# Low parts of the dense weights: an accumulating DMA in place of a subtraction on VectorE

## The chip, the cores and the metric

The kernel runs on one core of a Trainium2 chip. The metric is the time of one execution on the device, in microseconds. The core has five engines with a queue of instructions each, and every queue is worked through in order: TensorE (PE in the profile, with its weight loads as PEld), VectorE (DVE), ScalarE (ACT), GpSimd (POOL) and SyncE (SP), which here only issues DMAs. Sixteen DMA engines move the data of all queues.

## The reference

One layer of a hybrid encoder, for 512 tokens of width 1024, all in float32. A normalised input is projected once to 11,272 columns, which feed two token mixers and two gates; each mixer's result is projected back, gated and summed, and a last projection is added to the input:

```python
h = rmsnorm(x, norm_w)
proj = jnp.einsum('bsd,de->bse', h, w_in) + b_in
(mq, mk, mv, mi, mf, mo, mz, sq, sk, sv, sz, gates) = jnp.split(proj, split_at, axis=-1)
...
qk = jax.nn.silu(causal_depthwise_conv(jnp.concatenate([mq, mk], axis=-1), conv_w, conv_b))
hm = mlstm_chunkwise(...)                      # 4 heads of 256
y_m = hm * jax.nn.sigmoid(mo) * jax.nn.silu(mz)
...
os_ = stick_breaking_attention(qs, ks_, ...)   # 8 heads of 128
y_s = os_ * jax.nn.silu(sz)
...
merged = (g_m * jnp.einsum('bse,ed->bsd', y_m, w_proj_m)
          + g_s * jnp.einsum('bse,ed->bsd', y_s, w_proj_s))
x = x + jnp.einsum('bsd,de->bse', merged, w_out)
```

## The kernel before

TensorE works on the type fp32r, which keeps fewer bits than float32. To keep the accuracy, every operand is split into a high part (the value, rounded by writing it as fp32r) and a low part (the value less the high part), and each product is three matmuls: high by high, high by low, low by high (`mm3`, lines 84 to 87, accumulating in PSUM). A product of two low parts is left out.

The dense projections are 112 units of work (`Unit`, line 94). A unit is one block of weights of 128 x 1024 elements, 512 KB. In a `chan_group` the block is eight tiles of 128 input rows by 128 output channels, which TensorE holds as weights while the 512 tokens stream through. In a `tok_group` it is two tiles of 128 rows by 512 columns, which stream while the tokens are held; four units make one group of 512 columns. Either way a unit is 24 matmuls of 128x512.

A unit passes through three steps. `load` (line 107) issues the DMA from SP into the staging tile `st` (tag `stg`, three buffers). `split` (line 111) takes tiles `wh` and `wl` (three buffers each) and calls the helper `split` of line 89: ACT copies `st` to `wh` (L90), then DVE writes `wl` as `st` less `wh` (L91). The helper is also used for other operands: transposed queries and keys, attention weights, the mixers' outputs and the merged tile. `mm` runs the 24 matmuls, in two halves.

The order of all instructions is written out by hand (`manual_schedule`); the loop at line 980 goes over the units. For unit c it issues, in this order: the evacuation of unit c-1 from PSUM (`evac`, on ACT and DVE); what was deferred to c; `ahead(c)`, which splits up to unit c+2 and loads up to unit c+4; the first half of c's matmuls; one step of each attention or mLSTM head that is under way (generators, `head`); the second half. In the mLSTM query and key groups an attribute `slow` puts `ahead(c)` before the evacuation. The first four units are split by a routine of their own (`first_split`), so 108 units go through `Unit.split`.

Around the dense units lie the steps that the prediction names. The query and key groups of the mLSTM end in a causal convolution (`qk_group` of `MPair`): ACT adds the bias (L621), DVE runs four taps (L624 and three times L626), ACT takes a sigmoid (L629), and two later units finish it (L632, L638, L642). An attention head's scores go through two sigmoids on ACT (L407, L411), two masks on POOL (L409, L412), a running product and a multiplication on DVE (L415, L416), and are transposed on TensorE (L440). An mLSTM head's weights are exponentials on ACT (L699), and its outputs are normalised by ACT copies (L748) before TensorE transposes them (L762). POOL also computes the row norms (L260, L261). No DMA is issued from POOL.

Of the kernel before, what the change touches and what calls it, by code (L numbers as in the profile page):

```python
# [11 lines left out]
AF = mybir.ActivationFunctionType  # L12
OP = mybir.AluOpType
# [21 lines left out]
def tile_hybrid_layer(  # L35
# [16 lines left out]
    nc = tc.nc  # L52
# [20 lines left out]
    def blk(tag, dt=F32, shape=(512,), name=None, p=128):  # L73

        where = mp if tag in MISC else sp
        return where.tile([p] + list(shape), dt, name=name or tag, tag=tag, bufs=BUFS[tag])
# [12 lines left out]
    def split(src, hi, lo):  # L89
        nc.scalar.activation(hi, src, AF.Copy)  # L90
        nc.vector.tensor_tensor(lo, src, hi.bitcast(F32), op=OP.subtract)  # L91


    class Unit:
# [16 lines left out]
        def split(self):  # L111
            self.wh = blk("wh", FR, self.shape)
            self.wl = blk("wl", FR, self.shape)
            split(self.st, self.wh, self.wl)

    units = []

# [187 lines left out]
    class SbSet:  # L305
# [70 lines left out]
        def head(self, h):  # L376
            hs = slice(h * 128, (h + 1) * 128)
            tr = []
            for name in ("q", "k"):
                tp = att_ps()  # L380
                for tb in range(TB):
                    nc.tensor.transpose(tp[:, tb * 128:(tb + 1) * 128], self.raw[name][tb][:, hs], ident)  # L382
                th = blk("qk", FR, name=name + "th")
                tl = blk("qk", FR, name=name + "tl")
                if name == "q":
                    nc.scalar.activation(th, tp, AF.Copy, scale=qkw)
                    nc.vector.scalar_tensor_tensor(tl, tp, qkw, th.bitcast(F32), op0=OP.mult, op1=OP.subtract)
                else:
                    split(tp, th, tl)
                tr.append((th, tl))  # L390
# [43 lines left out]
            def turn(js):  # L434
                tp = att_ps()
                at = 0
                for j in js:
                    n = T - j * 128
                    for i in range(j, TB):
                        nc.tensor.transpose(tp[:, at + (i - j) * 128:at + (i - j + 1) * 128],  # L440
                                            a_t[i][:, j * 128:(j + 1) * 128], ident)
                    at += n
                ap = blk("P5", FR, (2, 512), name="at_split")
                ah, al = ap[:, 0, :], ap[:, 1, :]
                split(tp[:, 0:at], ah[:, 0:at], al[:, 0:at])
                at = 0
                for j in js:
                    n = T - j * 128
                    a_parts[j] = ah[:, at:at + n], al[:, at:at + n]
                    at += n  # L450
# [140 lines left out]
    class MPair:  # L591
# [84 lines left out]
        def head(self, h):  # L676
# [27 lines left out]
            def score(js):  # L704
                sc = att_ps()
                at = 0
                for j in js:
                    lo = j * 128
                    for d in range(2):
                        mm3(sc[:, at:at + T - lo], kt[d][0][:, lo:lo + 128], kt[d][1][:, lo:lo + 128],  # L710
                            qt[d][0][:, lo:], qt[d][1][:, lo:], d == 0, d == 1)
                    at += T - lo
                o = P_OFF[js[0]]
                w = w_all[:, o:o + at]
                nc.vector.tensor_tensor(w, sc[:, 0:at], w, op=OP.mult)
                ph, pl = [t[:, o:o + at] for t in p_all]
                split(w, ph, pl)
                for j in js:
                    pp[j] = [t[:, P_OFF[j]:P_OFF[j] + T - 128 * j] for t in p_all]
# [325 lines left out]
```

## Time and profile before

| | |
|---|---|
| time, median of 2 runs | 719.12 us (718.85 to 719.39) |
| the profiled execution's own time | 720.13 us |
| its span | 718.4 us |
| granted TensorE clock, mean | 0.997 |
| TensorE busy | 709.8 us |
| VectorE busy | 424.5 us |
| ScalarE busy | 315.8 us |
| GpSimd busy | 93.5 us |
| DMA | 67.80 MB, mean 94 GB/s |

In the profile, L12 is line 12 of the kernel; where a helper records an operation, the line is the helper's, so the split of every operand is on L90 and L91 and is told apart by its tiles. A line of a group gives the line, the engine, the operation, the tiles written and read, the shape and the count, then the busy time in us and the mean of one in ns, then the engine's idle time just before and who ended it. A line of the timeline gives start and duration in us, and in brackets the idle time before. A line of the windows gives the stretch and its length, then busy time and count for PE, PEld, DVE, ACT and POOL, the granted clock, the share of the 16 DMA engines in use, and GB/s. A line of the waits gives who waited for whom, the total in us, the number of times and the longest. A line of the DMA issues ends with the median time from issue to landing.

### The profile page before, as it was taken

To read this page: it belongs to the slowest core of one execution; us is meant where nothing else is said; L and a number is where in the kernel's file an instruction comes from. 1 tells how busy PE (TensorE), PEld (TensorE's weight loads), DVE (VectorE), ACT (ScalarE), POOL (GpSimd) and SP (SyncE) were. 2 spreads that over 40 slices of the span, in tenths; PEclk is the share of its full clock that TensorE was granted. 3 is DMA by queue.
4 is the path that set the end of the run, shared out by engine and by line. 5 is a ranking of instruction groups with operands and counts; after the bars stand their busy time and mean duration, and the time that the engine had idled before them with its cause. 6 is when DMAs were issued, how large, how long until landed. Compare 5 with 4: busy or idle time off the path is not lost.

```text
span 718.4 us, 9058 instructions
## 1 busy us (share of the span) xinstructions
PE 709.8 (99%) x3356; PEld 593.1 (83%) x3356; DVE 424.5 (59%) x663; ACT 315.8 (44%) x601; POOL 93.5 (13%) x235
## 2 busy tenths in 40 slices
PE   7999999999999999999999999999999999999997
PEld 5888888888888888888888888888888888888886
DVE  5837886656487568279944737994343254556441
ACT  5245364476255544244475534447554343222210
POOL 5422022253022112000001110000112000000000
PEclk9999999999999999999999999999999999999999
DMA  6433332233323222333332233333223333333621
GB/s 239 133 103 81 109 86 77 69 95 92 99 62 87 58 86 62 102 91 97 101 94 59 63 99 88 91 100 89 74 59 89 89 91 97 104 88 89 234 89 58
DMA packets 91475, 67.80 MB, mean 94 GB/s; under 512 B 3470, under 2 KB 77608, under 8 KB 91432
## 3 DMA queue, kind: packets, MB, share of 16 engines
q1 hardware_dynamic: 91432, 67.23, 32.8%
q8 instruction: 26, 0.43, 0.2%
q14 instruction: 17, 0.14, 0.1%
HBM read 65.12 MB, written 2.10 MB: 94 GB/s over the span
## 4 chain that ended last, share of the span: by engine, by line
PE 97%; DMA 1%; DVE 1%; POOL 0%; SPq 0%; issue 0%; ACT 0%; DVEq 0%
PE dps L85 28%; PE dps L87 27%; PE dps L86 27%; PE aps L86 2%; PE aps L87 2%; PE aps L85 2%; PE aps L440 1%; PE aps L382 1%; DMA stg<-in_w_in_dram 1%; PE dps L934 1%; PE dps L932 1%; PE dps L933 1%; PE aps L735 1%; PE aps L736 1%; PE aps L737 1%; DVE fl L891 0%
## 5 line engine op out<-in xcount | busy, mean ns | idle before, releaser
L91 DVE TENSOR_TENSOR wl<-stg,wh 128x1024 fp32r<-128x1024 f32 x108 | 132.3, 1225 | 140.3 <-ACT wh L90 139.9
L85 PE MATMUL dps<-hh,wh 128*128 128x512 f32 x448 | 175.8, 392 | 0.0
L86 PE MATMUL dps<-hl,wh 128*128 128x512 f32 x448 | 174.6, 390 | 0.0
L87 PE MATMUL dps<-hh,wl 128*128 128x512 f32 x448 | 174.6, 390 | 0.0
L90 ACT ACTIVATE wh<-stg 128x1024 fp32r<-128x1024 f32 x108 | 113.6, 1052 | 95.3 <-PE dps L87 58.6
L87 PEld LDWEIGHTS dps<-hh,wl 128*128 128x128 f32 x448 | 84.1, 188 | 17.7
L85 PEld LDWEIGHTS dps<-hh,wh 128*128 128x128 f32 x448 | 84.2, 188 | 17.5 <-issue 1.0
L86 PEld LDWEIGHTS dps<-hl,wh 128*128 128x128 f32 x448 | 84.2, 188 | 16.6
L85 PE MATMUL dps<-wh,hh 128*128 128x512 f32 x224 | 88.3, 394 | 0.0
L87 PE MATMUL dps<-wh,hl 128*128 128x512 f32 x224 | 87.4, 390 | 0.0
L86 PE MATMUL dps<-wl,hh 128*128 128x512 f32 x224 | 87.4, 390 | 0.0
L87 PEld LDWEIGHTS dps<-wh,hl 128*128 128x128 f32 x224 | 42.1, 188 | 8.9
L86 PEld LDWEIGHTS dps<-wl,hh 128*128 128x128 f32 x224 | 42.1, 188 | 8.2
L85 PEld LDWEIGHTS dps<-wh,hh 128*128 128x128 f32 x224 | 42.1, 188 | 8.2
L626 DVE SCALAR_TENSOR_TENSOR acc<-tmp,vec,acc 128x511 f32<-128x511 f32 (+2 forms) x48 | 36.0, 750 | 1.7
L629 ACT ACTIVATE tmp<-acc 128x512 f32<-128x512 f32 x16 | 10.1, 633 | 50.2 <-DVE acc L626 50.2
L415 DVE TENSOR_TENSOR_SCAN om<-om 128x512 f32<-128x512 f32 (+3 forms) x32 | 27.9, 871 | 6.3 <-POOL om L409 6.3
L409 POOL TENSOR_SCALAR_AFFINE_SELECT om<-om 128x128 f32<-128x128 f32 x32 | 12.1, 378 | 134.5 <-ACT om L407 134.5
L90 ACT ACTIVATE at_split<-aps 128x384 fp32r<-128x384 f32 (+1 forms) x24 | 11.8, 525 | 36.8 <-PE aps L440 36.8
L688 POOL TENSOR_SCALAR_AFFINE_SELECT w_all<-om 128x128 f32<-128x128 f32 x16 | 4.1, 293 | 168.9 <-DVE om L683 168.9
L91 DVE TENSOR_TENSOR at_split<-aps,at_split 128x384 fp32r<-128x384 f32 (+1 forms) x24 | 13.7, 599 | 19.8 <-ACT at_split L90 19.8
L86 PE MATMUL dps<-wl,mgh 128*128 128x512 f32 x64 | 24.9, 389 | 0.0
(239 smaller groups left out, 1170.6 us busy)
## 6 DMA issues: line engine op xcount, KB each, us to landing
stg<-in_w_in_dram SPq DMA_DIRECT2D x87, 512.0 KB, 3.7
stg<-in_w_proj_s_dram SPq DMA_DIRECT2D x8, 512.0 KB, 3.7
stg<-in_w_proj_m_dram SPq DMA_DIRECT2D x8, 512.0 KB, 3.6
stg<-in_w_out_dram SPq DMA_DIRECT2D x8, 512.0 KB, 3.7
brow<-in_b_in_dram SPq DMA_DIRECT2D x8, 256.0 KB, 4.2
xr<-in_x_dram SPq DMA_DIRECT2D x8, 256.0 KB, 5.7
out_dram<-xr SPq DMA_DIRECT2D x7, 256.0 KB, 2.3
x<-in_x_dram SPq DMA_DIRECT2D x3, 512.0 KB
```

What stands on the lines that cost most here:

```text
L85: nc.tensor.matmul(ps, ah, bh, start=first, stop=False)
L86: nc.tensor.matmul(ps, ah, bl, start=False, stop=False)
L87: nc.tensor.matmul(ps, al, bh, start=False, stop=last)
L90: nc.scalar.activation(hi, src, AF.Copy)
L91: nc.vector.tensor_tensor(lo, src, hi.bitcast(F32), op=OP.subtract)
L382: nc.tensor.transpose(tp[:, tb * 128:(tb + 1) * 128], self.raw[name][tb][:, hs], ident)
L409: nc.gpsimd.affine_select(out=om[:, ts], in_=om[:, ts], compare_op=OP.is_gt, fill=1.0, base=0, channel_multiplier=1, pattern=[[-1, 128]])
L415: nc.vector.tensor_tensor_scan(back, back, back, 1.0, op0=OP.mult, op1=OP.bypass)
L440: nc.tensor.transpose(tp[:, at + (i - j) * 128:at + (i - j + 1) * 128], a_t[i][:, j * 128:(j + 1) * 128], ident)
L626: nc.vector.scalar_tensor_tensor(acc[:, j:], t[:, 0:T - j], cw(3 - j, ch), acc[:, j:], op0=OP.mult, op1=OP.add)
L629: nc.scalar.activation(t, acc, AF.Sigmoid)
L735: nc.tensor.matmul(nm[:, 0:258], ph, vh, start=j == 0, stop=False)
```

## The change

Only `Unit.split` changes. The high part is written as before. The low part is no longer a subtraction on DVE: ACT writes the tile `wl` with the negated input, rounded to fp32r as the high part is, and then a DMA issued from POOL adds the staging tile to it, element by element, in SBUF: `wl = st + (-wh)`. The helper `split`, the first four units and all other operands stay as they are.

```diff
         def split(self):
             self.wh = blk("wh", FR, self.shape)
             self.wl = blk("wl", FR, self.shape)
-            split(self.st, self.wh, self.wl)
+            nc.scalar.activation(self.wh, self.st, AF.Copy)
+            nc.scalar.activation(self.wl, self.st, AF.Copy, scale=-1.0)
+            nc.gpsimd.dma_start(out=self.wl, in_=self.st, accum_op=OP.add)
```

## The prediction

> **What bounds the kernel now.** I read the page's busy times and its chain of waits first, then the groups by line, the waits, and last the order of time around the weight splits.
>
> ```profile
> span 718.4 us, 9058 instructions
> ```
> ```profile
> PE 709.8 (99%) x3356; PEld 593.1 (83%) x3356; DVE 424.5 (59%) x663; ACT 315.8 (44%) x601; POOL 93.5 (13%) x235
> ```
> ```profile
> PE 97%; DMA 1%; DVE 1%; POOL 0%; SPq 0%; issue 0%; ACT 0%; DVEq 0%
> ```
>
> TensorE is busy for 709.8 of 718.4 us and is 97% of the chain. Whatever is taken off VectorE can win at most the 8.6 us in which TensorE stands still, 1.2%. The work that the change moves is off that chain; the question is how much of its cover it eats.
>
> ```profile
> L91 DVE TENSOR_TENSOR wl<-stg,wh 128x1024 fp32r<-128x1024 f32 x108 | 132.3, 1225 | 140.3 <-ACT wh L90 139.9 <-DMA xr<-in_x_dram 0.3
> L90 ACT ACTIVATE wh<-stg 128x1024 fp32r<-128x1024 f32 x108 | 113.6, 1052 | 95.3 <-PE dps L87 58.6 <-PE dps L86 31.5 <-issue 5.0
> ```
> ```profile
> SPq L109 <- DVE wl L91: 538.7, 96, 10.2
> ```
>
> 108 blocks of weights are split: a high part on ACT in 1.05 us, a low part on DVE in 1.23 us, right behind it. The split is two units ahead of its use, and ACT waits for TensorE (58.6 + 31.5 us) because wh and wl have three buffers each. The loads on SP wait for the subtraction, which frees the staging buffer.
>
> **The cover in a plain unit.** I take the time from the end of a wh copy to the first matmul that reads that block's wl; all of the new chain must fit in it.
>
> ```profile
> 616.05 1.06 ACT L90 ACTIVATE wh<-stg 128x1024 fp32r<-128x1024 f32 x1 [3.34 <-PE dps L86]
> ```
> ```profile
> 627.41 0.39 PE L87 MATMUL dps<-yh,wl 128*128 128x512 f32 x1
> ```
> ```profile
> 634.59 1.04 ACT L90 ACTIVATE wh<-stg 128x1024 fp32r<-128x1024 f32 x1
> ```
> ```profile
> 643.73 0.39 PE L87 MATMUL dps<-yh,wl 128*128 128x512 f32 x1
> ```
>
> The first pair is one block: 627.41 - 617.11 = 10.30 us of cover. The second pair is the block three units later, so a unit lasts (643.73 - 627.41)/3 = 5.44 us. There ACT first splits an evacuated tile, wh starts 2.2 us later against the unit, and the cover is 643.73 - 635.63 = 8.10 us.
>
> **Part by part.** Removed: 108 subtractions, 132.3 us of DVE (424.5 to 292). They are hidden today, so by themselves they give nothing. Added on ACT: 108 more copies with a scale of -1, of the same shape as L90; 108 x 1.05 = 113 us, ACT from 315.8 to 429. Added on POOL: 108 DMA issues, each waiting for the second copy. Added on the DMA engines: 108 accumulating moves of 512 KB.
>
> The accumulate, from its start on POOL to TensorE's release, has no row. The nearest are these:
>
> ```profile
> stg<-in_w_in_dram SPq DMA_DIRECT2D x87, 512.0 KB, 3.7
> ```
> ```profile
> 324.00:342.00 18.00, 18.00 (x81) 14.92 (x80) 16.44 (x23) 8.09 (x13) 0.00 (x0) 1.00 0.38 101
> ```
> ```profile
> 360.00:378.00 18.00, 18.00 (x79) 14.71 (x79) 7.36 (x9) 13.24 (x23) 1.03 (x4) 1.00 0.34 88
> ```
> ```profile
> 684.00:702.00 18.00, 18.00 (x82) 14.89 (x81) 6.26 (x7) 3.18 (x3) 0.00 (x0) 1.00 0.25 88
> ```
> ```profile
> L891 POOL TENSOR_TENSOR fl<-stg,fh 128x512 fp32r<-128x512 f32 x2 | 2.5, 1274 | 4.0 <-ACT fh L890 4.0
> ```
>
> A load of the same 512 KB lands in 3.7 us. In 324 to 342 the DMA share is 0.38 at 101 GB/s: 1818 KB (10^3), 3.47 loads, so 0.38 x 18/3.47 = 2.0 us of all 16 engines for one load, with short rows. In 684 to 702, where a weight row is four times as long, it is 0.25 x 18/3.02 = 1.5 us. The rest of the 3.7, 1.7 us, is fixed. The accumulate reads source and destination: two passes, and its rows are whole partitions, so I price 2 x 1.5 = 3.0 us. For the issue on POOL I take 1.3 us, what POOL needs for one tile of 128x512 (an estimate, by nearness only). A load is in flight in some of that time: half of its 2.0 us. Sum: 1.3 + 1.7 + 3.0 + 1.0 = 7.0 us. Ends: 3.7 (as one load, with a free issue) and 11.1 (two reads and a write, each as long as a whole load). I call it X.
>
> The Trainium skill, "DMA: Bandwidth & Descriptors", section on the anatomy of a DMA issued from GpSimd, fits one such DMA as about 2.0 us plus bytes over 436 GB/s. For two source streams of 512 KB that is an estimate of 4.4 us; no run here shows it, and the sum with it would be near 722 us.
>
> From the end of the wh copy the new chain needs the second copy (0.95 us, the spacing of two ACT copies seen below) and X: 7.95 us. In plain units 2.35 us are spare, in the late units 0.15: nothing is lost. The staging buffer is held longer: load 3.7 + two copies 2.0 + X 7.0 = 12.7 us of the 16.3 us that three units give, so the loads on SP stay hidden with 3.6 us spare; without it the loss would be that of X itself. DMA engines: 2.0 + 3.0 = 5.0 us per unit of 5.44, 92%, still under. POOL's queue: the issue stands behind the masks of the unit before, which are about done when ACT comes to the copy; queued behind it are the masks and row norms of the next unit, and their input comes from ACT instructions queued behind the same copy, so the wait itself holds up little. In 360 to 378, ACT's fullest stage, 13.24 + 3.3 x 1.05 = 16.7 of 18 us: full, not over.
>
> **Where the cover is short.** In the convolution stage ACT and DVE already run a loop of their own, slower than TensorE:
>
> ```profile
> 324.69 0.63 ACT L629 ACTIVATE tmp<-acc 128x512 f32<-128x512 f32 x1 [3.07 <-DVE acc L626]
> 325.23 1.04 ACT L90 ACTIVATE wh<-stg 128x1024 fp32r<-128x1024 f32 x1
> 326.18 0.67 ACT L621 ACTIVATE tmp<-dps,bvec 128x512 f32<-128x512 f32 x1
> 326.75 0.62 ACT L638 ACTIVATE mqh<-tmp 128x512 fp32r<-128x512 f32 x1
> 330.44 0.63 ACT L629 ACTIVATE tmp<-acc 128x512 f32<-128x512 f32 x1 [3.07 <-DVE acc L626]
> ```
> ```profile
> 326.30 1.22 DVE L91 TENSOR_TENSOR wl<-stg,wh 128x1024 fp32r<-128x1024 f32 x1 [0.26 <-ACT wh L90]
> 327.45 0.54 DVE L624 TENSOR_SCALAR acc<-tmp,vec 128x512 f32<-128x512 f32 x1
> ```
>
> Sigmoid to sigmoid is 5.75 us against 5.44. Now wh starts, 0.95 us later the biased copy L621, and DVE's L624 starts 327.45 - 325.23 = 2.22 us after wh, behind the subtraction. After the change L621 starts 1.90 us after wh and ends at 2.57; L624 follows at 2.60. The subtraction goes, the second copy is late next, and the loop becomes 5.75 + 0.38 = 6.13 us. Eight loops are 3.0 us of lateness on top of today's. The last block behind them in each of the two stages:
>
> ```profile
> 361.12 1.04 ACT L90 ACTIVATE wh<-stg 128x1024 fp32r<-128x1024 f32 x1
> ```
> ```profile
> 369.23 0.39 PE L87 MATMUL dps<-hh,wl 128*128 128x512 f32 x1
> ```
> ```profile
> 487.45 1.04 ACT L90 ACTIVATE wh<-stg 128x1024 fp32r<-128x1024 f32 x1
> ```
> ```profile
> 495.95 0.39 PE L87 MATMUL dps<-hh,wl 128*128 128x512 f32 x1
> ```
>
> Cover 7.07 and 7.46 us; less 3.0 it is 4.07 and 4.46 against 7.95 needed: TensorE stalls 3.9 + 3.5 = 7.4 us. Two more places:
>
> ```profile
> 581.39 1.05 ACT L90 ACTIVATE wh<-stg 128x1024 fp32r<-128x1024 f32 x1
> ```
> ```profile
> 589.33 0.39 PE L87 MATMUL dps<-ysh,wl 128*128 128x512 f32 x1
> ```
> ```profile
> 541.83 1.05 ACT L90 ACTIVATE wh<-stg 128x1024 fp32r<-128x1024 f32 x1
> 542.78 0.83 ACT L748 ACTIVATE hns<-aps,hst 128x256 f32<-128x256 f32 x2
> ```
> ```profile
> 543.77 0.49 PE L762 MATMUL aps<-ident,hns 128*128 128x128 f32 x3
> ```
>
> At 589.33 the cover is 6.89: 1.1 us short. The copies L748 end at 543.61, 0.16 us before TensorE transposes them; a copy of 0.95 us slipped in ahead costs 0.8. Sum 7.4 + 1.1 + 0.8 = 9.3 us. The profiled execution took 720.1 us (718.4 of span and 1.7 around it): 729.4. The median of the runs, 719.1, is 1.0 lower: 728.4. I say 729.
>
> With X at 3.7 the sum is 0.8 + 0.8 = 1.6 us (721). With 11.1 the chain needs 12.05 and plain units stall too: 12.05 - 10.30 = 1.75 us per two units. The plain stretches are 306 to 360, 432 to 486 and 576 to 718 us, 250 us or 46 units: 40 us, and with the short places some 45 (764).
>
> The Trainium skill, "SBUF — State Buffer", section on who interferes with whom, speaks against the change: a VectorE instruction in a two-port mode, and a scalar-tensor form such as L624 can be one, locks GpSimd out while it writes descriptors. In the convolution loop that could add up to L624's 0.54 us to X, about 1.1 us to the sum; the trace of before issues no DMA from POOL and cannot show it.
>
> **The rivals.** (1) All hidden, 719 to 724: X under 5.5, as a load's 3.7 suggests. Against it: two passes, and a load beside it. The estimate from the Trainium skill's fit falls here too. (2) Slower by more than 2%: the accumulate paces plain units. Once X exceeds 10.30 - 0.95 = 9.35, each further us costs half a us in each of 46 units; or the DMA engines are full, if a move takes three passes: 2.0 + 4.5 = 6.5 us per unit, 46 x 1.06 = 49 us, 767. For it: 92% already; against it: long rows. Between 7.8 and 9.35 the late units (0.15 spare, eight of them, half a us each per us) join the convolution stage: 734 to 750. (3) VectorE's relief wins something: bounded by TensorE's 8.6 us of idle time. In the two rows that follow, the first and last 18 us of the span, TensorE is busy for 13.66 of 18.00 and 12.16 of 16.40 us: all of the idle time lies there, away from nearly all of these splits, and 2% is out of reach. (4) The move goes element by element and not by partition rows: far beyond 800; loads of 512 KB here do not, so I give it a few hundredths inside (2).
>
> ```profile
> 0.00:18.00 18.00, 13.66 (x46) 9.88 (x47) 10.69 (x19) 10.68 (x19) 9.04 (x19) 0.91 0.68 239
> ```
> ```profile
> 702.00:718.40 16.40, 12.16 (x54) 9.76 (x52) 2.83 (x5) 0.00 (x0) 0.00 (x0) 0.97 0.17 64
> ```
>
> **How the numbers follow.** Forecast (X 5.5 to 7.8, 724 to 733.5) 0.37; hidden 0.18; 733.5 to 750 0.18; above 750 0.25; faster by 2% 0.02. Two per cent, about what a measurement of this kernel can tell from no change, is 14.4 us, reached at X near 7.8. So faster 0.02, same 0.55, slower 0.43. The range 721 to 775 leaves out under a tenth below and about a tenth above; the likeliest case alone spans 724 to 733.5.
>
> **What would show it.** X: the time to landing of the new DMA in the list of DMA issues. TensorE's waits: none at plain units, some for that DMA near 370, 496 and 589 us. ACT's sigmoid spacing in the convolution stage: 6.13 us. Sub-steps are wrong if POOL's masks get late enough to stall the transposes of the attention weights, if ACT falls behind outside these stages, or if SP's loads become the last thing waited for. The prediction is wrong if X is above 9.35 us or the DMA share passes 0.95.

## The result and the profile after

The changed kernel takes 727.84 us (727.77 to 727.90, 2 runs) against 719.12 us: a ratio of 1.0123, with a 95% interval of 1.0104 to 1.0141. It is 8.7 us slower: clear of noise, but inside the 2% that the prediction called no change.

The page of the changed kernel (span; busy time and share by engine; the chain by engine; the software queue that POOL issues to; the new DMA, with its median time to landing):

```profile
span 726.1 us, 9291 instructions
...
PE 711.0 (98%) x3356; PEld 590.9 (81%) x3356; DVE 297.2 (41%) x555; ACT 416.8 (57%) x709; POOL 186.9 (26%) x343
...
q0 software_dynamic: 15552, 56.63, 41.0%
...
PE 75%; DMA 7%; issue 6%; DVE 5%; ACT 5%; POOL 1%; SPq 0%; ACTq 0%; DVEq 0%; POOLq 0%
...
wl<-stg POOLq DMA_DIRECT2D x108, 512.0 KB, 5.4
```

VectorE lost 127 us of work and ScalarE gained 101; neither number is on the clock. What is, is that TensorE now waits for the new DMA, which it never did for the subtraction. The waits of PE in the changed kernel (who waited for whom, total us, times, longest):

```profile
PE dps L86 <- DMA wl<-stg: 4.1, 3, 1.7
PE dps L87 <- DMA wl<-stg: 2.9, 4, 1.4
```

Seven waits, 7.0 us, and some more around each, since the weight loads just before them wait too. To place the loss I took the start of the first matmul of each unit from both traces. From unit 4 to unit 111 the changed kernel loses 9.3 us: 2.7 between units 44 and 56 and 1.1 between 64 and 76, which are the two convolution stages, and 5.6 from unit 88 on, nearly all of it from unit 104. Everywhere else the differences are below 0.05 us. That this span is longer by only 7.7 us comes of the start: in the profiled execution of before the first weight load landed 1.4 us later, as the chain of waits shows, before in the first block of lines and changed in the second (start, duration):

```profile
2.52 6.75 DMA stg<-in_w_in_dram
```
```profile
2.56 5.33 DMA stg<-in_w_in_dram
```

The convolution stage of the changed kernel, ACT in order of time (L114 is now the wh copy, L115 the negated copy, L623 the bias, L631 the sigmoid), then POOL and PE:

```profile
324.07 0.64 ACT L631 ACTIVATE tmp<-acc 128x512 f32<-128x512 f32 x1 [2.51 <-DVE acc L628]
324.61 1.04 ACT L114 ACTIVATE wh<-stg 128x1024 fp32r<-128x1024 f32 x1
325.56 1.04 ACT L115 ACTIVATE wl<-stg 128x1024 fp32r<-128x1024 f32 x1
326.51 0.67 ACT L623 ACTIVATE tmp<-dps,bvec 128x512 f32<-128x512 f32 x1
327.08 0.62 ACT L640 ACTIVATE mqh<-tmp 128x512 fp32r<-128x512 f32 x1
330.21 0.63 ACT L631 ACTIVATE tmp<-acc 128x512 f32<-128x512 f32 x1 [2.51 <-DVE acc L628]
```
```profile
365.09 0.86 POOL L116 DMA_DIRECT2D wl<-stg  x1 [6.58 <-ACT wl L115]
```
```profile
370.40 0.50 PE L87 MATMUL dps<-hh,wl 128*128 128x512 f32 x1 [1.38 <-DMA wl<-stg]
```

Sigmoid to sigmoid is 6.14 us. At the block behind the last loop TensorE stands still, and unit 55 loses 1.7 us: the block's DMA is issued at 365.09 and released the matmul at 370.40, 5.3 us later. The other 1.0 us of this stage is lost earlier, inside the loops, at unit 50, where one accumulate took 7.8 us to land:

```profile
333.03 0.94 POOL L116 DMA_DIRECT2D wl<-stg  x1 [5.19 <-ACT wl L115]
```
```profile
340.84 0.50 PE L87 MATMUL dps<-hh,wl 128*128 128x512 f32 x1 [0.72 <-DMA wl<-stg]
```

At the end the DMA engines are nearly full (columns as before; the last number but one is their share), and the chain of waits runs through transfers that release each other:

```profile
648.00:666.00 18.00, 17.84 (x79) 14.43 (x78) 6.91 (x10) 8.78 (x11) 2.59 (x3) 1.00 0.90 189
666.00:684.00 18.00, 16.71 (x74) 13.51 (x73) 4.15 (x6) 7.73 (x9) 3.45 (x4) 1.00 0.92 233
684.00:702.00 18.00, 15.15 (x66) 11.88 (x65) 2.77 (x4) 5.91 (x6) 2.59 (x3) 1.00 0.93 233
```
```profile
666.96 8.04 DMA wl<-stg
675.05 0.37 SPq L109
675.52 4.17 DMA xr<-in_x_dram
679.76 12.34 DMA stg<-in_w_out_dram
692.17 2.33 issue
694.51 5.68 DMA wl<-stg
```

An accumulate that takes 8.04 us holds a staging buffer; SP, in its order, waits for that buffer, then issues one weight load, then the residual loads (`xr`), then the next weights, which need 12.34 us; their accumulate follows, and TensorE stands for it. The share alone does not explain this: the same view shows 0.94 in a stretch in which no unit loses anything:

```profile
612.00:630.00 18.00, 18.00 (x81) 14.92 (x80) 4.93 (x8) 7.70 (x9) 2.59 (x3) 1.00 0.94 199
```

### The profile page after: what moved, and what is told of

It is laid out like the page before. It is cut to its first block, busy times and chain, and to the rows that moved or that the text cites. A ratio compares the mean times of both kernels' runs of the same rounds, so it can differ in the third digit from the quotient of the medians.

```text
span 726.1 us, 9291 instructions
## 1 busy us (share of the span) xinstructions
PE 711.0 (98%) x3356; PEld 590.9 (81%) x3356; DVE 297.2 (41%) x555; ACT 416.8 (57%) x709; POOL 186.9 (26%) x343
## 4 chain that ended last, share of the span: by engine, by line
PE 75%; DMA 7%; issue 6%; DVE 5%; ACT 5%; POOL 1%; SPq 0%; ACTq 0%; DVEq 0%; POOLq 0%
PE dps L87 20%; PE dps L85 20%; PE dps L86 20%; DMA wl<-stg 4%; DVE acc L628 3%; PE aps L86 2%; PE aps L87 2%; PE aps L85 2%; ACT wl L115 2%; ACT wh L114 2%; DMA stg<-in_w_out_dram 2%; PE aps L442 1%; PE aps L384 1%; PE dps L936 1%; PE dps L934 1%
## 5 line engine op out<-in xcount | busy, mean ns | idle before, releaser
L116 POOL DMA_DIRECT2D wl<-stg x108 | 96.0, 889 | 450.4 <-ACT wl L115 432.6
L114 ACT ACTIVATE wh<-stg 128x1024 fp32r<-128x1024 f32 x108 | 113.7, 1052 | 81.8 <-PE dps L87 43.8
L115 ACT ACTIVATE wl<-stg 128x1024 fp32r<-128x1024 f32 x108 | 112.8, 1044 | 0.0
L631 ACT ACTIVATE tmp<-acc 128x512 f32<-128x512 f32 x16 | 10.1, 633 | 41.2 <-DVE acc L628 41.2
L87 PE MATMUL dps<-yh,wl 128*128 128x512 f32 x64 | 25.0, 391 | 0.2 <-DMA wl<-stg 0.2
L87 PE MATMUL dps<-wh,mgl 128*128 128x512 f32 x64 | 25.0, 390 | 0.0
```

Of the source, the lines that this page charges most:

```text
L87: nc.tensor.matmul(ps, al, bh, start=False, stop=last)
L114: nc.scalar.activation(self.wh, self.st, AF.Copy)
L115: nc.scalar.activation(self.wl, self.st, AF.Copy, scale=-1.0)
L116: nc.gpsimd.dma_start(out=self.wl, in_=self.st, accum_op=OP.add)
L631: nc.scalar.activation(t, acc, AF.Sigmoid)
```

## Experiments

Every edit is shown against the changed kernel, except for the two controls on the kernel before. Theory A, after the two traces: the loss has two causes. In the convolution stage the second ACT copy makes the ACT and DVE loop longer, so that blocks start late and the accumulate no longer fits in the cover. At the end, the accumulates, the weight loads and the residual loads crowd the DMA engines, so that landings get long. The rival, theory B: one cause, the load that the accumulates put on the DMA engines, and where TensorE stalls is only where the cover happens to be short.

The table gives, for each kernel, what its unit starts lose against the profiled execution of before (us, by stage), and the median of the runs. It is worked out from the start of the first matmul of units 44, 56, 64, 76, 88, 104 and 111. Each row is one execution. In the six kernels that leave the convolution stages as the change has them (changed, the three on the residual loads, no change of type, last blocks subtracted) these two stages together lose between 3.8 and 6.4 us, so differences of a us or two between two rows need not come of the edit.

| kernel | units 44-56 | 64-76 | 88-104 | 104-111 | time, us |
|---|---|---|---|---|---|
| changed | 2.7 | 1.1 | 0.5 | 5.1 | 727.84 |
| negation on VectorE | 0.0 | 0.0 | 0.1 | 2.8 | 721.34 |
| plain move | 0.3 | 0.0 | 0.0 | 0.8 | 719.79 |
| residual loads earlier | 2.4 | 1.5 | 4.5 | 0.0 | 726.92 |
| no change of type | 2.7 | 1.3 | 0.5 | 6.3 | 728.36 |
| residual loads spread | 2.4 | 4.0 | 2.2 | 2.3 | 728.83 |
| last blocks subtracted | 2.9 | 1.9 | 0.0 | 0.0 | 724.25 |
| no residual loads | 2.5 | 1.3 | 1.3 | 0.8 | 724.92 |
| both removed | 0.0 | 0.0 | 0.0 | 0.0 | 718.81 |

**Negation on VectorE.** One part of the change undone: the extra copy leaves ACT.

```diff
-            nc.scalar.activation(self.wl, self.st, AF.Copy, scale=-1.0)
+            nc.vector.tensor_scalar(self.wl, self.st, -1.0, None, op0=OP.mult)
```

> The negated copy into wl moves from ACT to DVE; the accumulating DMA stays. Theory A (the second ACT copy stretches the convolution loop to 6.13 us, and that lateness plus the 5.4 us of the accumulate uses up the cover): sigmoid to sigmoid falls to about 5.2 to 5.5 us, TensorE no longer stalls between 306 and 380 or 432 and 505 us, the 3.7 us lost there come back, and the accumulate starts up to 1 us earlier everywhere, so some of the 5.6 us lost after 640 us comes back too: 721 to 724.5 us. Theory B (the DMA engines' load sets the loss, whichever engine writes the negation): 727 to 729 us, stalls in the same places.

Measured: 721.34 us, ratio 1.0031 (1.0019 to 1.0042). ACT in the same stage:

```profile
323.77 1.06 ACT L114 ACTIVATE wh<-stg 128x1024 fp32r<-128x1024 f32 x1
324.74 0.67 ACT L623 ACTIVATE tmp<-dps,bvec 128x512 f32<-128x512 f32 x1
325.31 0.62 ACT L640 ACTIVATE mqh<-tmp 128x512 fp32r<-128x512 f32 x1
328.45 0.63 ACT L631 ACTIVATE tmp<-acc 128x512 f32<-128x512 f32 x1 [2.52 <-DVE acc L628]
329.21 1.07 ACT L114 ACTIVATE wh<-stg 128x1024 fp32r<-128x1024 f32 x1
```

From wh copy to wh copy the loop is back to 5.44 us, TensorE's pace, and both convolution stages lose nothing, with the same DMAs and bytes. Theory B expected 727 to 729 us; for this stage it is out. The negation on DVE takes 690 ns against 1.04 us on ACT, and it need not wait for the wh copy, so accumulates start earlier elsewhere too; the end, from unit 88 on, still loses 2.9 us.

**Plain move.** The price of the accumulate itself: the same DMA without the addition. The low part is then the whole weight, so this kernel leaves the correction out.

```diff
-            nc.gpsimd.dma_start(out=self.wl, in_=self.st, accum_op=OP.add)
+            nc.gpsimd.dma_start(out=self.wl.bitcast(F32), in_=self.st)
```

> The DMA from POOL copies st over wl instead of adding to it, so the low part is wrong (it is the whole weight): one source stream in place of two, same bytes written, same issue, same copies on ACT. If two source streams set the price: 16 engines' time per move falls from 2.76 us to 1.4 to 1.5, the shortest time to landing from 4.4 to about 3.1, the median to about 3.8, and of the 9.3 us of stalls 2 to 4 are left: 721 to 723 us. If the fixed part of the move rules: time to landing within 0.5 us of 5.4 and 726 to 728 us.

Measured: 719.79 us, ratio 1.0013 (1.0004 to 1.0022). Its queue, its time to landing and its issue on POOL, against 41.0%, 5.4 us and 889 ns:

```profile
q0 software_dynamic: 15552, 56.63, 19.6%
...
wl<-stg POOLq DMA_DIRECT2D x108, 512.0 KB, 2.9
```
```profile
L116 POOL DMA_DIRECT2D wl<-stg x108 | 59.7, 553 | 468.5 <-ACT wl L115 450.1 <-PE dps L87 7.5 <-PE aps L87 6.7
```

With the same count of packets and bytes, a move occupies the 16 engines for 0.196 x 718.2/108 = 1.30 us; the accumulate for 0.410 x 726.1/108 = 2.76 us, 2.1 times as much. With 2.5 us less to landing, almost all of the loss goes, more than expected, although ACT's loop is as long as in the changed kernel (6.14 us). So the convolution loss needs both, the late start and the long landing.

**No change of type.** The plain move differs in a second thing: it writes float32. This run tells the two apart.

```diff
-            nc.gpsimd.dma_start(out=self.wl, in_=self.st, accum_op=OP.add)
+            nc.gpsimd.dma_start(out=self.wl.bitcast(F32), in_=self.st, accum_op=OP.add)
```

> The accumulating DMA writes its tile as float32 in place of fp32r (same bytes, no change of type; TensorE reads the same tile). If the second source stream is what doubles a move (1.31 us of 16 engines for the plain move, 2.76 for the accumulate): nothing changes, shortest time to landing 4.4 us, median 5.3 to 5.5, software queue at 41%, 727 to 728.5 us. If the change of type is part of it: median below 4.5 us, share below 35%, 722 to 726 us.

Measured: 728.36 us, ratio 1.0130 (1.0113 to 1.0147); queue 40.9%, landing 5.3 us. The type costs nothing; the price is the addition together with its second source. The Trainium skill, "Collectives: The Full Stack", section on the bandwidth ceiling, says of a reduction step between cores that it is half as fast as a copy because it reads two sources and not because of the addition; the 2.1 agrees with the half, and no run here tells the two reasons apart.

**Residual loads earlier**, and the same in the kernel before as a control:

```diff
-    later.setdefault(n_proj, []).append(load_xr(0))
-    later.setdefault(n_proj, []).append(load_xr(1))
+    later.setdefault(n_gates + 9, []).append(load_xr(0))
+    later.setdefault(n_gates + 12, []).append(load_xr(1))
```

> The eight loads of the residual (xr, 2 MB) are issued 7 and 4 units earlier (before units 97 and 100 instead of both before unit 104). Theory A (after 660 us these loads collide with the accumulates: one landed in 9.4 us, one weight load in 12.3 us): TensorE's stalls after unit 104 (1.6 + 1.4 + 2.1 us) go, with perhaps 1 us new near units 97 to 102: 722.5 to 724.5 us. Theory B (the late stage is short only because ACT reaches wh 2.2 us late there, and the accumulates' own spread does the rest): 727 to 728.5 us.

> The kernel before with the same earlier residual loads, as control: TensorE waits for no load there, so both theories expect no change, 718.5 to 719.7 us.

Measured: 726.92 us, ratio 1.0104 (1.0087 to 1.0121); the control 718.94, ratio 0.9997 (0.9988 to 1.0006). The stalls moved with the loads: units 104 to 111 lose nothing, units 99 to 104 lose 4.5 us. So the collision is real, but the time fell by 0.9 us only, where I had expected 3 to 5. The trace shows one reason: unit 102 alone loses 4.2 us, of which 2.35 us are the wait, and right behind it the granted clock was about half for 3.4 us, in which matmuls start every 0.43 us instead of every 0.23 (the wait, then the window):

```profile
665.41 0.50 PE L87 MATMUL dps<-yh,wl 128*128 128x512 f32 x1 [2.35 <-DMA wl<-stg]
```
```profile
665.90:669.30 3.40, 3.40 (x10) 2.70 (x9) 0.00 (x0) 1.59 (x2) 0.86 (x1) 0.51 0.79 196
```

Half the clock for 3.4 us costs some 1.7 us, an estimate; without it the stage from unit 88 on would lose 2.8 us instead of the changed kernel's 5.6. The run whose clock stayed at 1.000 took 725.15 us, the other three, at 0.995 to 0.999, 726.87 to 727.15.

**Residual loads spread**, one at a time (`load_xr` is changed to load one tile):

```diff
...
-    later.setdefault(n_proj, []).append(load_xr(0))
-    later.setdefault(n_proj, []).append(load_xr(1))
+    for i, at in enumerate((9, 11, 13, 15, 17, 18, 19, 20)):
+        later.setdefault(n_gates + at, []).append(load_xr(i // 4, i % 4))
```

> The changed kernel with the eight residual loads issued one at a time (before units 97, 99, 101, 103, 105, 106, 107, 108) instead of all before unit 104. A unit then needs 2.0 (weights) + 2.8 (accumulate) + 0.75 (256 KB of residual) = 5.5 us of the 16 engines in the units that have one, against 5.44 us, and 4.8 in those between. Theory A (2 MB at once collide with the accumulates): the 5.5 us of stalls after unit 99 fall to 1 to 2.5: 723.5 to 725.5 us. Theory B (units from 99 on are short by the late wh alone): 726.5 to 728 us.

Measured: 728.83 us (726.06 to 730.88), ratio 1.0136 (1.0107 to 1.0165): nothing won in the median. The end loses 4.5 us in six small stalls in place of 5.6 in a few large ones, where theory A expected 1 to 2.5: this expectation fell. The 4.0 us in units 64 to 76 lie before any of the moved loads. They are for the most part one pause of 2.1 us with 3.4 us at half the clock behind it, as above, so the profiled execution's total says little of the edit; the run at a clock of 1.000 took 726.06 us. So the burst makes a small part of the loss at the end at most; that the sum of the work makes the rest is argued, not shown.

**No residual loads.** The tiles are set to zero instead, so the input is not added at the end.

```diff
-                nc.sync.dma_start(xr[g][tb], xf[tb * 128:(tb + 1) * 128, g * 512:(g + 1) * 512])
+                nc.vector.memset(xr[g][tb], 0.0)
```

> The changed kernel without the eight loads of the residual; the tiles are set to zero, so x is not added at the end. All accumulates stay. If the residual's 2 MB are what overfills the DMA engines late: stalls after unit 99 fall from about 5.5 to at most 1 us, 722.5 to 724.5 us. If accumulates and weight loads alone do it: 726 to 728.5 us.

Measured: 724.92 us, ratio 1.0076 (1.0061 to 1.0091). Of the 5.6 us from unit 88 on, 2.1 are left. So the residual's 2 MB make some 3.5 us of it; the rest comes about without them, from the accumulates and the weight loads. That it falls on these units because wh starts late there is argued from the 8.10 us of cover and was not tested by itself. Neither of the two expectations holds alone.

**Last blocks subtracted.** No accumulate from block 98 on:

```diff
-        def split(self):
+        def split(self, low_on_dve):
             self.wh = blk("wh", FR, self.shape)
             self.wl = blk("wl", FR, self.shape)
+            if low_on_dve:
+                return split(self.st, self.wh, self.wl)
...
-            units[count["ready"]].split()
+            units[count["ready"]].split(count["ready"] >= 98)
```

> The changed kernel, but blocks 98 to 111 get their low part by the subtraction on VectorE as before: no accumulate in the last stage, the rest unchanged. Theory A (the late stalls come of the DMA engines' work, accumulates beside weight and residual loads): no stall after unit 98, those in the convolution stay at 3 to 5 us: 722 to 724.5 us. Theory B (something else that the change does late, such as ACT's fuller queue): 726 us or more.

Measured: 724.25 us, ratio 1.0062 (1.0044 to 1.0080). The waits of PE for the DMA that are left are all in the convolution stages:

```profile
PE dps L87 <- DMA wl<-stg: 3.9, 3, 1.6
```

**Both removed.** Negation on VectorE and the last blocks subtracted; 94 blocks still go through the accumulating DMA.

```diff
...
-            nc.scalar.activation(self.wl, self.st, AF.Copy, scale=-1.0)
+            nc.vector.tensor_scalar(self.wl, self.st, -1.0, None, op0=OP.mult)
...
-            units[count["ready"]].split()
+            units[count["ready"]].split(count["ready"] >= 98)
```

> Negation on VectorE (as in the first experiment) and blocks 98 to 111 by subtraction; 94 blocks still go through the accumulating DMA. Theory A (the two causes are the second ACT copy in the convolution loop and the crowded DMA engines at the end, and nothing else): no stall is left and the time is that of the kernel before, 718.5 to 719.7 us. If the accumulates cost something by themselves: 720.5 us or more.

Measured: 718.81 us, ratio 0.9997 (0.9987 to 1.0007). All waits of PE in this kernel; none is for the DMA, and all lie in the first units:

```profile
PE dps L936 <- DVE hh L292: 1.5, 1, 1.5
PE dps L914 <- DVE idle L909: 1.5, 1, 1.5
PE dps L938 <- DVE fl L895: 0.7, 1, 0.7
PE aps L290 <- DVE x L280: 0.5, 1, 0.5
```

Between them the second copy on ACT and the accumulates of the last stage account for the whole loss, and the 94 accumulates that stay cost nothing. They win nothing either: 50 us less work on DVE, the same time. What this run does not show is how much of the loss at the end is the crowded engines and how much the short cover, since it takes the accumulates of that stage away altogether.

**One unit ahead instead of two**, in the changed kernel and in the one before. This takes away cover and leaves every instruction, DMA and byte as it is.

```diff
-AHEAD, LOADS = 2, 4
+AHEAD, LOADS = 1, 4
```

> Split one unit ahead instead of two: the cover falls by one unit, 10.3 to about 4.9 us in plain units, while instructions, DMAs and bytes stay the same. Theory A (cover against copy 0.95 + issue 0.3 + landing of at least 4.4 us sets TensorE's pace): a unit cannot be shorter than about 1.0 + 1.0 + 0.3 + 4.4 to 5.0 - 0.4 = 6.3 to 7.0 us, with wh late in some more; the unit starts of the changed kernel then add 50 to 100 us: 775 to 830 us. Theory B (the load of the DMA engines sets the loss, not the time ahead): within 10 us of 728.

> The kernel before with the split one unit ahead, as control: copy 1.05 + subtraction 1.23 = 2.3 us of 4.9 us of cover in plain units, so nearly unchanged, 719 to 726 us, the loss where ACT or DVE are late already (convolution, late units).

Measured: 822.34 us, ratio 1.1439 (1.1416 to 1.1462), and 719.33 us, ratio 1.0005 (0.9995 to 1.0016). With the change, the waits of PE and the first line of the page's busy times:

```profile
PE dps L87 <- DMA wl<-stg: 47.3, 36, 4.5
PE dps L86 <- DMA wl<-stg: 19.6, 14, 4.0
```
```profile
PE 745.2 (91%) x3356; PEld 602.0 (73%) x3356; DVE 297.6 (36%) x555; ACT 415.8 (51%) x709; POOL 186.3 (23%) x343
```

The queue of the accumulates is less full than in the changed kernel (35.4% of the engines against 41.0%), they land sooner (4.6 us against 5.4 in the median), and the unit starts lose eleven times as much, 103.9 us from unit 4 to unit 111. This is the clearest evidence that the time ahead, not the engines' share, is what hides an accumulate. The subtraction's 2.3 us fit in either.

## Why the prediction was right, and where it was not

The forecast was 729 us and no change by the 2% rule; 727.84 was measured, well inside the likeliest case. The sum of the stalls was forecast at 9.3 us and came out at 9.3. That agreement is luck in good part: the terms do not agree one by one. With X, the time from the second copy's end to TensorE's release, as it was measured, the forecast's own sum would have been 2.5 + 2.1 + 0 + 0.8 = 5.4 us, or 724.5; what makes up the rest are stalls at the end, which it put at nothing. Nor is 2% what a measurement here can tell: the interval puts a change of 1.2% clear of none.

- **TensorE as the bound, nothing to win from VectorE:** right. The kernel with both causes removed frees VectorE of 50 us at no stall and gains nothing.
- **The loop of 6.13 us:** right, 6.14 us, and by the step that was given: the subtraction goes, the second copy is late next.
- **The convolution term, 7.4 us:** right stages and mechanism, size off by half: 3.8 (2.7 + 1.1). X was the mis-sized term. I took 7.0 us from the copy's end; measured is 0.3 us to the issue plus a median of 5.4 (4.4 at the shortest, 9.4 at the longest). The parts: issue 0.89 against 1.3, two streams 2.76 against 3.0, and what is left of the shortest landing, 4.4 - 0.89 - 2.76 = 0.7, against 1.7, which I had carried over from a load from HBM. In the first stage the last block needed 0.95 + 0.3 + 5.3 = 6.55 against 4.07 of cover, which gives 2.5; the 2.7 were lost in two pieces, because the 1.0 us at unit 50 had already given the loop that much time back. In the second stage the last block's landing was one of the short ones, 4.4 us: 5.65 needed against 4.46 gives 1.2, and 1.1 was lost.
- **The 1.1 us at 589 us:** the same error of X; the unit loses 0.03 us.
- **The 0.8 us at the transposes L762:** wrong. In the changed kernel these run while the copies before them are still going, without a wait (L750 and L764 there):

```profile
546.09 0.83 ACT L750 ACTIVATE hns<-aps,hst 128x256 f32<-128x256 f32 x2
```
```profile
546.13 1.03 PE L764 MATMUL aps<-ident,hns 128*128 128x128 f32 x8
```

  Two heads are under way there, and the copies belong to the other one: in the code two copies in one step stand near a head's start, while the transposes come one step behind a head's single last copy. The profile leaves out buffer numbers; I paired two lines by a tile's name.
- **The late units, "nothing is lost":** wrong, 5.6 us. The step that failed is the DMA engines' share, "92%, still under", with 0.15 us of cover to spare. It was an average of a plain unit, it left out the residual's 2 MB, and it used one X for all blocks, where landings spread from 4.4 to 9.4 us.
- **The loads on SP, hidden with 3.6 us spare:** right except at the end, where the queue on SP carries the delay from one transfer to the next: it waited for accumulates 104 times, 622 us in total, and one weight load needed 12.3 us, for which ACT stood 9.6 us before the longest stall of TensorE.
- **POOL's queue and ACT in the attention stages:** right. ACT's fullest stage rose to 15.9 of 18 us, and units 4 to 44 lose 0.0 us.
- **Slower, the accumulate paces plain units:** did not happen, X stayed under 9.35 us except for one landing of 9.4 us, which with the 0.3 before it makes 9.7. The experiment with one unit ahead shows the mechanism at work.
- **The fit of 4.4 us in the Trainium skill ("DMA: Bandwidth & Descriptors", section on the anatomy of a DMA issued from GpSimd):** it agrees with the shortest landing, 4.4 us; the median is 1.0 above it. With it alone the forecast would have been 722 us.
- **GpSimd locked out by L624:** the issue takes 0.95 us in the convolution loop, where that instruction runs beside it, and 0.86 outside. The lock, if it is that, costs 0.09 us and not 0.54; no run here shows whether L624 works in a two-port mode at all.

## What to carry to other kernels

Work moved off an engine that is not the bottleneck onto a longer path costs nothing as long as the time ahead covers it: measure for each stage the time between the first step of the chain and the first use, and subtract the new chain; here 10.3 us hid 6.6, and 4.9, one unit of 5.4 less, did not. Price an accumulating DMA at about twice a plain move (2.1 times here), and look for the stages where other transfers come at the same time, because a landing there can double (4.4 to 9.4 us here) while the mean share looks no worse than where nothing is lost (0.92 and 0.94). And when an operation leaves one engine, ask which in-order loop the work that replaces it joins: one more copy of 0.95 us on ACT lengthened a loop by 0.39 us, and taking it out again on a faster engine gave back the whole loss of that stage.

## What the runs showed of the hardware

- An accumulate of 512 KB within SBUF holds the 16 DMA engines for 2.76 us, a plain move of the same bytes for 1.30; POOL needs 0.89 us to issue the one and 0.55 the other. A destination of fp32r or float32 makes no difference (41.0% and 40.9%).
- The shortest landing hardly varies (4.36 to 4.38 us in all kernels with the accumulate), while the longest lies between 7.7 and 10.4 us. Most of the spread goes with the other transfers: in the changed kernel the 15 accumulates beside which other queues used under 0.1 us of the 16 engines took 4.6 us on average, the 20 with 2.5 us or more 7.1.
- Some pauses of TensorE cost more than their length. In three kernels (residual loads earlier, spread, no change of type) a pause of 2.1 to 2.4 us was followed by 3.4 us at half the granted clock; pauses of up to 1.9 us in these, and all in the changed kernel (up to 1.7), were not. The limit does not hold strictly: with one unit ahead two pauses of 2.3 and 2.5 us were not followed by it either. There the granted clock averaged 0.971, and the busy time of the same 3356 matmuls rose from 711.0 to 745.2 us. Of the 94.8 us by which that span is longer than the changed kernel's, 59.9 are longer waits for the accumulates and 34.2 longer busy time; the stretches at half the clock, 47.8 us in all, account for some 24 of these 34 by estimate.
- POOL's one-element fills `om` went from 98 ns on average to 316 with the accumulates issued beside them, and its first mask from 378 to 468. With plain moves issued from POOL in the same places they took 108 and 317 ns, so issuing DMAs is not enough to cause it. TensorE never waited for them, and the cause stays open.
